# Block sums of the MLP weights: by DMA additions from DRAM to DRAM during the attention, instead of by GpSimd during merge and MLP

## The chip, the cores and the metric

One NeuronCore of one Trainium2 chip runs the whole program. The metric is device microseconds of one execution, the median of several runs.

## The reference

One layer of a decoder in float32, with S = D = 1024 and DFF = 4096:

```python
h = rms_norm(x);  proj = h @ w_in          # q k v | conv x,B,C | q_m | 3 gates
y_attn = (differential attention, 8 heads, causal) @ w_attn_o
y_conv = (B * causal conv3(C * x_c)) @ w_conv_o
y_mem  = (cross attention over 256 memory rows) @ w_mem_o
x = x + (g_a*y_attn + g_c*y_conv + g_m*y_mem) @ w_o
h2 = rms_norm(x, norm_mlp_g)
x = x + square(relu(h2 @ w_mlp_in)) @ w_mlp_out
```

## The kernel before

Every float32 product is made as three TensorE (PE) matmuls of rounded parts: each operand is split into hi (a cast, `whi`, `whh`, on ACT) and lo (raw minus hi, `wlo`, on DVE or GpSimd/POOL), and hi·hi, hi·lo, lo·hi are added up. A weight is so first loaded into a "raw" tile by SP's queue, then split, then used.

The program in order of time in the profiled execution:

- 0 to 245 us: memory attention and the norm of x.
- 245 to 1256: the attention, 64 steps s (8 heads of 8 row blocks). Each step issues the score, transpose and value products of a block, and `qkv(s + 1)` (L648 to L676), whose small norm chain on POOL is sq, r (two instructions, in `rstd_of`), qd; the transposes of qd are PE's next work for that block. Between these pieces PE runs matmuls of a stream (`fill_steps`), the conv and gate projections of x. At a change of head, `load_head` loads and casts the next head's weights (`rawh`, then `whh`).
- 1256 to 1536: the merge, three branches b = 2, 1, 0 of eight columns (`branch_steps`). At the last column of a branch `prep` loads and splits the next branch's operand (`rawx`, then `x`); at the very last, the first third of W_o.
- 1536 to 1632: W_o and the residual; 1632 to 1731: the row norm, and the transposes for the MLP.
- 1731 to 1997: the MLP's first product (`up`), and to 2314 the second. Each is a 2x2 block scheme of the Strassen family: seven block products instead of eight for each of 8 groups g. Of the seven weight blocks of each product four are sums of quarters of the weight matrix. The operands X are made by `second_sums` and `put`; the first product's results are squared (`out1`), combined and stored to `u_dram`, which the second product reads.

The weight sums are made by the program itself. `sum_jobs` (L530) has 32 jobs for w_mlp_in: two SP loads of 256 KB into one tile `sumw` of the "raw" pool (three buffers, shared with every `raw`, `rawh` and `rawx`), four POOL additions or subtractions, a 512 KB store from POOL's queue to `sw1_dram`. Eight are called in the attention (one in each head, at s % 8 == 6), 24 in the merge (L618, after each column's second half). `sum_jobs2` (L547) does the same for w_mlp_out, 32 jobs beside `up`, in the three "t" buffers that `tt` and `tu` use.

What sets the order: PE's instructions are pinned in the order of the program, and so are all SP loads (`pin_load`). The order on DVE, ACT and POOL is made by the tile framework's scheduler, which may put an instruction earlier than it is written.

Of the kernel before, what the change touches and what calls it, by code (L numbers as in the profile page):

```python
# [60 lines left out]
def tile_hybrid_block(ctx: ExitStack, tc: tile.TileContext, x, mem, norm_mix_g, norm_mem_g, w_in, b_gate,  # L61
# [103 lines left out]
    def row(name, src, n):  # L165
        t = const.tile([P, n], F32, name=name)
        nc.scalar.dma_start(t, src.unsqueeze(0).broadcast_to([P, n]))
        return t

    def rstd_of(ss, n, width, tag):  # L170

        r = sm.tile([P, width], F32, tag=tag, bufs=3, name="r")
        G.tensor_scalar(r, ss, 1.0 / n, EPS, op0=ALU.mult, op1=ALU.add)  # L173
        G.tensor_tensor(out=r, in0=r, in1=mhalf[:, 0:width], op=ALU.pow)  # L174
        return r


# [109 lines left out]
    z_dram = dram.tile([3, KT, P, S], F32, name="z_dram")  # L287

    NG = DFF // 512
    sw1_dram = dram.tile([NG, P, 4, 4, 256], F32, name="sw1_dram")  # L290
    sw2_dram = dram.tile([NG, P, 4, 2, 512], F32, name="sw2_dram")


    memT = [[slot(f"memT{c}{kq}", shape=(P, 4, MEM)) for kq in range(2)] for c in "hl"]
# [229 lines left out]
                yield  # L524


    def sub_(out, a, b):
        G.tensor_tensor(out=out, in0=a, in1=b, op=ALU.subtract)  # L528

    def sum_jobs():  # L530

        w1b = w_mlp_in.rearrange("(h k p) (c g n) -> h k p c g n", h=2, k=4, p=P, c=2, n=256)
        for g in range(NG):
            for k in range(4):
                z = rawt("sumw", (P, 2, 2, 256))
                for h in range(2):
                    load(z[:, h], w1b[h, k, :, :, g, :])
                a11, a21, a12, a22 = z[:, 0, 0], z[:, 0, 1], z[:, 1, 0], z[:, 1, 1]
                G.tensor_tensor(out=a22, in0=a21, in1=a22, op=ALU.add)  # L539
                sub_(a21, a11, a21)  # L540
                sub_(a11, a22, a11)
                sub_(a12, a12, a11)

                G.dma_start(sw1_dram[g, :, :, k, :], z.rearrange("p a b n -> p (a b) n"))
                yield

    def sum_jobs2(tile):  # L547
        w2b = w_mlp_out.rearrange("(h g j p) (d m n) -> h g j p d m n", h=2, j=2, p=P, d=2, n=256)
        for g in range(NG):
            for j in range(2):  # L550
                for m in range(2):
                    z = tile().rearrange("p a (b n) -> p a b n", b=2)
                    for h in range(2):
                        load(z[:, h], w2b[h, g, j, :, :, m, :])
                    b11, b12, b21, b22 = z[:, 0, 0], z[:, 0, 1], z[:, 1, 0], z[:, 1, 1]
                    sub_(b11, b12, b11)
                    sub_(b12, b22, b12)
                    sub_(b22, b22, b11)
                    sub_(b21, b21, b22)

                    G.dma_start(sw2_dram[g, :, :, j, m * 256:(m + 1) * 256], z.rearrange("p a b n -> p (a b) n"))
                    yield
# [33 lines left out]
    def branch_steps(b):  # L596
        w_src = srcs[b][0]
        w, z = ready.pop(b)
        for c in range(KT):
            gt = rowt("gt")  # L600
            load(gt, z_dram[b, c])
            A.activation(gt, gt, AF.Sigmoid, bias=bg[:, b * KT + c:b * KT + c + 1])
            wn = load_w(w_src[:, (c + 1) * P:(c + 2) * P], P, "wh", V) if c + 1 < KT else None
            if b == 2:
                merged[c] = slot("merged", F32, tag="m")
            if c == KT - 1:
                if b:
                    prep(b - 1)
                else:
                    ready["wo"] = load_wo(0)  # L610
            if b == 0:
                mh, ml = mT.add("mT", ("fw" if c < 4 else "s", "m" if c else "s"))
            for hf in range(2):
                sl = slice(hf * 512, (hf + 1) * 512)
                ps = ps_sc(512) if hf else ps_mm()
                yield from mm3_steps(ps, w, z.half(hf))
                if hf:
                    run(jobs, 1)  # L618
                if b == 2:
# [220 lines left out]
    for s in range(ns):  # L840

        if s == 0:
            fill = (16, 8, 8, 1)
        elif s == ns - 1:
            fill = (10, 40, 10, 8)
        else:
            fill = (17, 7, 8, 4)
        qk_transposes(s)
        run(stream, fill[0])
        if s == 0:  # L850
            p_transposes(nq - 1)
# [12 lines left out]
        values(s)  # L864
        if s % 8 == 6:
            run(jobs, 1)
        run(stream, fill[3])
    run(stream, 24)
# [135 lines left out]
    def second_sums(t):  # L1004
        ra, rb = rows.pop(t - 4), rows.pop(t)
        tt, tu = blk("tt", "t"), blk("tu", "t")
        sub(G, tt[:, 0], rb[:, 0], ra[:, 0])
        sub(V, tu[:, 0], rb[:, 1], rb[:, 0])
        sub(G, tt[:, 1], rb[:, 1], tt[:, 0])
        sub(G, tu[:, 1], ra[:, 1], tt[:, 1])  # L1010
        tsum[t] = rb, tt, tu

    def second_half(t):
# [6 lines left out]

    B = {}

    def out1(g, name, src, addend=None):

        t = B[g, name] = blk(name, "c")
        if addend is None:
            A.activation(t, src, AF.Relu)
            V.tensor_tensor(out=t, in0=t, in1=t, op=ALU.mult)
        else:
            add(V, t, src, addend)  # L1030
            V.scalar_tensor_tensor(out=t, in0=t, scalar=0.0, in1=t, op0=ALU.max, op1=ALU.mult)
# [6 lines left out]
    def up(n):  # L1038
# [16 lines left out]
            out1(g, "c11", ps, B.pop((g, "s", 1)))  # L1055
            put_u(1, g, B[g, "c11"])
        if i == 7:
            out1(g, "c22", ps1[g, "Z"], B.pop((g, "s", 7)))
            put_u(4, g, B[g, "c22"])
        if i == 4:  # L1060
            out1(g, "c21", ps)
            put_u(2, g, B[g, "c21"])
        if i == 3:
            out1(g, "c12", ps, B.pop((g, "s", 6)))
            c11, c12, c21, c22 = (B.pop((g, c)) for c in ("c11", "c12", "c21", "c22"))

            add(V, c22, c12, c22)
# [13 lines left out]
        first_half(t)  # L1081
    split1(1)
    alloc_x(6, 5, 7, 4, 3)
    jobs = sum_jobs2(lambda: blk("sumw", "t"))
    for n in range(len(seq1)):
        if 9 < n < 48 and n % 7 != 3:
            run(jobs, 1)
        load1(n + 4)
        split1(n + 2)
        if n < 4:  # L1090
            load_rows(n)
            load_rows(4 + n)
            second_sums(4 + n)
        up(n)
        if n < 4:
            second_half(4 + n)

    run(jobs)


    w2v = w_mlp_out.rearrange("(h g j p) (d n) -> h d g p j n", h=2, j=2, p=P, d=2)
# [3 lines left out]
    def load2(n):  # L1105
        if n < len(seq2):
# [4 lines left out]
            if i in (1, 2, 3):  # L1111
                h, d = {1: (0, 0), 2: (1, 0), 3: (1, 1)}[i]
                load(w, w2v[h, d, g])
            else:
                load(w, sw2_dram[g, :, {5: 0, 7: 1, 4: 2, 6: 3}[i]])

    def split2(n):
        if n < len(seq2):
# [24 lines left out]
    for n, (i, g) in enumerate(seq2):  # L1143
# [7 lines left out]
        for m in range(4):  # L1151
# [4 lines left out]
                             stop=g == NG - 1 and k == 1 and q == 2, skip_group_check=True)  # L1156
            if i == 3 and g == NG - 1:
                t = sn[6][m // 2]
                add(V, t[:, m % 2, :], ps[m // 2][:, m % 2, :], t[:, m % 2, :])
                put_out(0, 1, m // 2, t, (m % 2,))  # L1160
        if g < NG - 1:
            continue
# [51 lines left out]
```

## Time and profile before

| | |
|---|---|
| median of 3 runs | 2313.75 us (2308.81 to 2314.91) |
| the profiled execution | 2315.68 us |
| its span in the profile | 2313.9 us |
| PE busy | 2219.8 us (96%) |
| DVE, ACT, POOL busy | 1213.6, 953.1, 811.6 us |
| bytes moved by DMA | 338.29 MB, mean 146 GB/s |

PE is busy nearly throughout, so a shorter time needs fewer idle stretches of PE, or less time at its lower clock, and a row on another engine counts only where PE waits for it. The granted clock ("PEclk") is 1.00 at 2.4 GHz; a window of time that shows 0.75 ran half of its time at 1.2 GHz.

### The profile page before, as it was taken

The page shows a single profiled execution, that of the slowest core. Times are in us where ns is not written, and L with a number is a line of the kernel's source. Part 1 is how long each engine was busy: PE and PEld are TensorE (multiplying, and loading weights), DVE is VectorE, ACT ScalarE, POOL GpSimd, SP SyncE. Part 2 cuts the span into 40 slices and gives each one's busy share as a digit, 9 for nine tenths or more (in the row PEclk, how much of TensorE's full clock was granted, in tenths as well). Part 3 has the DMA queues.
Part 4 walks back from the last instruction along what each step waited for, and adds up shares of the span by engine and source line. Part 5 has one row for each costly group of instructions (what it writes and reads, how often), then busy time and mean ns, then how long its engine had stood idle before and what let it go on. Part 6 is the DMA issues. An engine that isn't in the chain of part 4 may idle for free.

```text
span 2313.9 us, 31608 instructions
## 1 busy us (share of the span) xinstructions
PE 2219.8 (96%) x11472; PEld 1919.3 (83%) x11472; DVE 1213.6 (52%) x2200; ACT 953.1 (41%) x2190; POOL 811.6 (35%) x1084
## 2 busy tenths in 40 slices
PE   6999999999999999999999999989679999999999
PEld 6999888888888888888887887879568888788887
DVE  6755455555555555555556343342447676664452
ACT  5544445454545454444545232331222323354341
POOL 5422233333233232333334444641417788100000
PEclk9999999999999999999999999999789999999999
DMA  7412121222212121222214775752828999886660
GB/s 201 128 61 63 46 79 59 67 80 66 72 51 91 42 87 42 75 63 67 80 64 143 238 238 174 226 157 90 294 83 307 331 338 350 292 304 219 219 227 37
DMA packets 242748, 338.29 MB, mean 146 GB/s; under 512 B 20256, under 2 KB 182048, under 8 KB 242592
## 3 DMA queue, kind: packets, MB, share of 16 engines
q1 hardware_dynamic: 206128, 239.64, 32.5%
q0 software_dynamic: 19584, 71.31, 8.2%
q10 hardware_dynamic: 16880, 25.33, 3.1%
q8 instruction: 90, 1.47, 0.3%
q14 instruction: 66, 0.54, 0.1%
HBM read 235.56 MB, written 100.66 MB: 145 GB/s over the span
## 4 chain that ended last, share of the span: by engine, by line
PE 74%; DMA 10%; DVE 6%; POOL 4%; issue 3%; ACT 2%; SPq 1%; ACTq 0%; POOLq 0%; DVEq 0%
PE ps_mm L89 37%; PE X L89 14%; PE Z L89 11%; PE ps_sc L89 7%; DMA sumw<-in_w_mlp_in_dram 3%; PE ps_tr L93 3%; PE ps_tr L89 3%; POOL sumw L528 2%; DVE wlo L184 1%; DMA raw<-in_w_attn_o_dram 1%; DMA xr<-xn_dram 1%; SPq L98 1%; POOL merged L623 1%; DMA sw_dram<-sumw 1%; POOL sumw L539 1%
## 5 line engine op out<-in xcount | busy, mean ns | idle before, releaser
L89 PE MATMUL ps_mm<-hT,whi 128*128 128x512 f32 x1536 | 490.3, 400 | 1.7 <-DVE vst L668 1.7
L89 PEld LDWEIGHTS ps_mm<-hT,whi 128*128 128x128 f32 x1536 | 279.0, 189 | 53.3 <-DVE vst L668 4.7
L89 PE MATMUL ps_mm<-hT,wlo 128*128 128x512 f32 x768 | 301.7, 393 | 0.0
L89 PE MATMUL ps_mm<-whh,hT 128*128 128x384 f32 x1024 | 276.4, 340 | 1.9 <-DVE inner L475 1.9
L528 POOL TENSOR_TENSOR sumw<-sumw 128x256 f32<-128x256 f32 x224 | 215.0, 961 | 40.5 <-DMA sumw<-in_w_mlp_out_dram 29.6
L89 PEld LDWEIGHTS ps_mm<-whh,hT 128*128 128x128 f32 x1024 | 186.3, 188 | 7.2 <-DVE inner L475 3.7
L184 DVE TENSOR_TENSOR wlo<-raw,whi 128x256 fp32r<-128x256 f32 (+2 forms) x169 | 123.9, 749 | 121.4 <-ACT whi L202 108.6
L89 PE MATMUL X<-w,u 128*128 128x512 f32 x768 | 174.6, 389 | 0.0
L184 POOL TENSOR_TENSOR wlo<-raw,whi 128x512 fp32r<-128x512 f32 (+2 forms) x95 | 116.3, 1230 | 162.9 <-ACT whi L202 161.9
L89 PE MATMUL ps_mm<-whl,hT 128*128 128x384 f32 x512 | 171.4, 335 | 0.0
L89 PEld LDWEIGHTS X<-w,u 128*128 128x128 f32 x768 | 144.2, 188 | 29.9
L670 POOL TENSOR_TENSOR sq<-qk 128x256 f32<-128x256 f32 x64 | 42.6, 665 | 356.9 <-ACT qk L665 356.5
L89 PEld LDWEIGHTS ps_mm<-hT,wlo 128*128 128x128 f32 x768 | 144.7, 188 | 27.5
L202 ACT CAST whi<-raw 128x512 fp32r<-128x512 f32 (+2 forms) x264 | 127.0, 530 | 77.5 <-PE ps_mm L89 13.1
L174 POOL TENSOR_TENSOR r<-r,mhalf 128x1 f32<-128x1 f32 (+1 forms) x186 | 132.8, 714 | 14.4
L914 DVE TENSOR_TENSOR u<-uraw,u 128x1024 fp32r<-128x1024 f32 x56 | 72.1, 1288 | 118.9 <-ACT u L920 118.5
L89 PE MATMUL Z<-w,u 128*128 128x512 f32 x576 | 131.7, 390 | 1.6 <-DVE snap L917 1.6
L173 POOL TENSOR_SCALAR r<-ss 128x1 f32<-128x1 f32 (+1 forms) x186 | 39.7, 214 | 255.2 <-ACT ps_tr L764 106.0
L89 PEld LDWEIGHTS Z<-w,u 128*128 128x128 f32 x576 | 108.0, 188 | 24.8 <-DVE snap L917 2.4
L89 PE MATMUL ps_mm<-x,whi 128*128 128x512 f32 x384 | 120.6, 395 | 4.0 <-DVE x L184 3.3
L920 ACT CAST u<-uraw 128x1024 fp32r<-128x1024 f32 x56 | 59.0, 1054 | 156.9 <-PE X L89 74.6
L89 PE MATMUL ps_sc<-x,whi 128*128 128x512 f32 x384 | 118.8, 391 | 1.1 <-DVE gt L622 1.1
(236 smaller groups left out, 4836.1 us busy)
## 6 DMA issues: line engine op xcount, KB each, us to landing
sw_dram<-sumw POOLq DMA_DIRECT2D x64, 512.0 KB, 5.8
raw<-in_w_in_dram SPq DMA_DIRECT2D x56, 512.0 KB, 3.8
u_dram<-c POOLq DMA_DIRECT2D x56, 512.0 KB, 6.0
uraw<-u_dram SPq DMA_DIRECT2D x56, 512.0 KB, 5.3
sumw<-in_w_mlp_in_dram SPq DMA_DIRECT2D x64, 256.0 KB, 4.1
w1raw<-sw_dram SPq DMA_DIRECT2D x32, 512.0 KB, 6.6
sumw<-in_w_mlp_out_dram SPq DMA_DIRECT2D x64, 256.0 KB, 6.0
w2raw<-sw_dram SPq DMA_DIRECT2D x32, 512.0 KB, 4.3
```

Source lines behind the costliest of these rows:

```text
L89: return cls.pin(nc.tensor.matmul(*a, **kw))
L93: return cls.pin(nc.tensor.transpose(*a, **kw))
L98: return pin_load(nc.sync.dma_start(dst, src))
L173: G.tensor_scalar(r, ss, 1.0 / n, EPS, op0=ALU.mult, op1=ALU.add)
L174: G.tensor_tensor(out=r, in0=r, in1=mhalf[:, 0:width], op=ALU.pow)
L184: eng.tensor_tensor(out=lo, in0=raw, in1=f(hi), op=ALU.subtract)
L202: A.copy(out=hi[:, a:b, :], in_=raw[:, k0 + a:k0 + b, :])
L528: G.tensor_tensor(out=out, in0=a, in1=b, op=ALU.subtract)
L539: G.tensor_tensor(out=a22, in0=a21, in1=a22, op=ALU.add)
L670: G.tensor_tensor(out=sq, in0=qk, in1=qk, op=ALU.mult)
L914: eng.tensor_tensor(out=out, in0=a, in1=b, op=ALU.subtract)
L920: A.copy(out=hl[:, 0], in_=raw)
```

## The change

All 64 jobs go. In their place POOL's queue issues 16 DMAs of 4.19 MB each (a quarter of a weight matrix) from DRAM to DRAM, eight plain copies and eight additions (`accum_op` add: the destination gets source plus destination). One is issued every third step of the attention, at s = 1, 4, ..., 46, and pinned behind the last `pow` that has been written (`last_norm`). Each matrix needs four sums; each begins as a copy of a quarter or of an earlier sum, and quarters are added to it:

| s | 1 | 4 | 7 | 10 | 13 | 16 | 19 | 22 |
|---|---|---|---|---|---|---|---|---|
| w_mlp_in | copy r to z0 | copy r to z1 | add s to z0 | add q to z1 | copy z0 to z2 | add q to z2 | copy z2 to z3 | add t to z3 |

and w_mlp_out the same way at s = 25 to 46 (its additions to z0 and z1 are q and s, its z2 begins as z1). Rows are 8 KB for w_mlp_in, 2 KB for w_mlp_out, and 64 KB where both sides are whole sums. A DMA that reads or adds to what an earlier one wrote waits for it, and the wait stands on POOL, which issues it.

Only sums can be made so, no differences; the signs are moved to other operands: `put` negates two of the X blocks, and a few additions become subtractions. The loads of the sums into `w1raw` now have runs of 1 KB where they had 4 KB. `load_w` in `branch_steps` no longer names DVE for all of the lo parts, so they alternate between DVE and POOL.

```diff
     def rstd_of(ss, n, width, tag):
...
-        G.tensor_tensor(out=r, in0=r, in1=mhalf[:, 0:width], op=ALU.pow)
+        last_norm[0] = G.tensor_tensor(out=r, in0=r, in1=mhalf[:, 0:width], op=ALU.pow)
...
-    sw1_dram = dram.tile([NG, P, 4, 4, 256], F32, name="sw1_dram")
-    sw2_dram = dram.tile([NG, P, 4, 2, 512], F32, name="sw2_dram")
+    sw1 = [dram.tile([D // 2, DFF // 2], F32, name=f"sw1{i}") for i in range(4)]
+    sw2 = [dram.tile([DFF // 2, D // 2], F32, name=f"sw2{i}") for i in range(4)]
...
     def sum_jobs():
 
-        w1b = w_mlp_in.rearrange("(h k p) (c g n) -> h k p c g n", h=2, k=4, p=P, c=2, n=256)
-        for g in range(NG):
-            for k in range(4):
-                z = rawt("sumw", (P, 2, 2, 256))
...
+        def go(out, in_, op=ALU.bypass):
+            after(G.dma_start(out, in_, accum_op=op), last_norm[0])
+
+        a = [w_mlp_in[h * 512:(h + 1) * 512, c * 2048:(c + 1) * 2048] for c in range(2) for h in range(2)]
+        b = [w_mlp_out[h * 2048:(h + 1) * 2048, d * 512:(d + 1) * 512] for h in range(2) for d in range(2)]
+        for (q, t, r, s), z in ((a, sw1), ((b[0], b[2], b[1], b[3]), sw2)):
+            for i, src, op in ((0, r, 0), (1, r, 0), (0, s, 1), (1, q if z is sw1 else s, 1), (2, z[0 if z is sw1 else 1], 0),
+                               (2, q, 1), (3, z[2], 0), (3, t, 1)):
+                if z is sw2 and (i, op) == (0, 1):
+                    src = q
+                go(z[i], src, ALU.add if op else ALU.bypass)
                 yield
...
-            wn = load_w(w_src[:, (c + 1) * P:(c + 2) * P], P, "wh", V) if c + 1 < KT else None
+            wn = load_w(w_src[:, (c + 1) * P:(c + 2) * P], P, "wh") if c + 1 < KT else None
...
-                if hf:
-                    run(jobs, 1)
...
-        if s % 8 == 6:
+        if s % 3 == 1:
             run(jobs, 1)
...
-                load(r, sw1_dram[g, :, {6: 0, 7: 1, 3: 2, 5: 3}[i]])
+                load(r, sw1[{5: 0, 7: 1, 6: 2, 3: 3}[i]].rearrange("(k p) (g n) -> g p k n", p=P, n=256)[g])
...
-        A.copy(out=hi, in_=src)
-        sub(V, lo, src, f(hi))
+        if i in (4, 5):
+            A.activation(hi, src, AF.Copy, scale=-1.0)
+            V.scalar_tensor_tensor(out=lo, in0=src, scalar=-1.0, in1=f(hi), op0=ALU.mult, op1=ALU.subtract)
+        else:
+            A.copy(out=hi, in_=src)
+            sub(V, lo, src, f(hi))
...
-            sub(V, c11, c22, c11)
-            sub(V, c21, c21, c11)
+            V.scalar_tensor_tensor(out=c11, in0=c22, scalar=-1.0, in1=c11, op0=ALU.mult, op1=ALU.subtract)
+            V.scalar_tensor_tensor(out=c21, in0=c21, scalar=-1.0, in1=c11, op0=ALU.mult, op1=ALU.subtract)
...
-    jobs = sum_jobs2(lambda: blk("sumw", "t"))
     for n in range(len(seq1)):
-        if 9 < n < 48 and n % 7 != 3:
-            run(jobs, 1)
```

The order moves at three places. First POOL inside a step of the attention, before: four `sumw` operations of a job stand between the members of the norm chain (sq, r, r, qd).

```order
L539 TENSOR_TENSOR sumw<-sumw 128x256
L670 TENSOR_TENSOR sq<-qk 128x256
L528 TENSOR_TENSOR sumw<-sumw 128x256
L173 TENSOR_SCALAR r<-ss_3891 128x4
L528 TENSOR_TENSOR sumw<-sumw 128x256
L174 TENSOR_TENSOR r<-r,mhalf 128x4
L528 TENSOR_TENSOR sumw<-sumw 128x256
L675 TENSOR_TENSOR qd<-qk,r 128x256
L544 DMA sw_dram<-sumw 512x1x256
```

The same place after, around one of the 16 DMAs (`sw_92`): the chain sq, r, r, qd has nothing between, and the DMA stands behind the next norm and ahead of the next step's sq.

```order
L648 TENSOR_TENSOR sq<-qk 128x256
L175 TENSOR_SCALAR r<-ss_6043 128x4
L176 TENSOR_TENSOR r<-r,mhalf 128x4
L653 TENSOR_TENSOR qd<-qk,r 128x256
L186 TENSOR_TENSOR wlo<-raw,whi 128x512
L175 TENSOR_SCALAR r<-ss 128x1
L176 TENSOR_TENSOR r<-r,mhalf 128x1
L532 DMA sw_92<-in_w_mlp_in_dram 512x2048
L648 TENSOR_TENSOR sq<-qk 128x256
```

What moved: the job's arithmetic is gone, and one DMA issue, which may carry a wait for an earlier DMA, stands ahead of sq. Second ACT at the change of head in step s = 14, before: the casts of the next head's weights (`whh`) come among the exponentials `e` of that step.

```order
L777 ACTIVATE osl<-ps_tr,sg 128x128
L644 CAST whh<-rawh 128x384
L723 ACTIVATE e,sums<-ps_sc,negm 128x896
L644 CAST whh<-rawh 128x384
L723 ACTIVATE e,sums<-ps_sc,negm 128x896
L644 CAST whh<-rawh 128x384 x2
L665 COPY qk<-ps_mm 128x256
L667 CAST vst<-ps_mm 128x128
L644 CAST whh<-rawh 128x384
```

After, the casts but the first come behind the whole step:

```order
L622 CAST whh<-rawh 128x384
L701 ACTIVATE e,sums<-ps_sc,negm 128x896 x2
L643 COPY qk<-ps_mm 128x256
L645 CAST vst<-ps_mm 128x128
L724 CAST aT<-ps_tr 128x512
L724 CAST aT<-ps_tr 128x384
L502 COPY z<-ps_mm 128x512
L739 ACTIVATE o<-ps_tr,sums 128x128
```

What moved: three or more `whh` casts that stood ahead of the step's `qk` copy now stand behind its `o`. Third POOL at the end of the merge, before: `sumw` operations and a store stand between the last additions into `merged`, which W_o reads.

```order
L544 DMA sw_dram<-sumw 512x1x256
L623 TENSOR_TENSOR merged<-merged,gt 128x512 x3
L539 TENSOR_TENSOR sumw<-sumw 128x256
L623 TENSOR_TENSOR merged<-merged,gt 128x512
L528 TENSOR_TENSOR sumw<-sumw 128x256 x3
L544 DMA sw_dram<-sumw 512x1x256
L623 TENSOR_TENSOR merged<-merged,gt 128x512 x2
```

After:

```order
L601 TENSOR_TENSOR merged<-merged,gt 128x512 x2
L186 TENSOR_TENSOR wlo<-raw,whi 128x384
L601 TENSOR_TENSOR merged<-merged,gt 128x512 x2
L186 TENSOR_TENSOR wlo<-raw,whi 128x384
L186 TENSOR_TENSOR wlo<-raw,whi 128x256
L601 TENSOR_TENSOR merged<-merged,gt 128x512 x7
L186 TENSOR_TENSOR wlo<-raw,whi 128x384 x4
```

What moved: nothing but the `wlo` parts that `load_w` now gives to POOL stands between the last `merged` additions.

## Rows read from the trace of the kernel before

**Rows 1.** The profile page, parts 1, 2 and 3 (queue: packets, MB, share of 16 engines).

```profile
PE 2219.8 (96%) x11472; PEld 1919.3 (83%) x11472; DVE 1213.6 (52%) x2200; ACT 953.1 (41%) x2190; POOL 811.6 (35%) x1084
...
PEclk9999999999999999999999999999789999999999
...
GB/s 201 128 61 63 46 79 59 67 80 66 72 51 91 42 87 42 75 63 67 80 64 143 238 238 174 226 157 90 294 83 307 331 338 350 292 304 219 219 227 37
...
q0 software_dynamic: 19584, 71.31, 8.2%
```

**Rows 2.** Windows: us, busy (xcount) of PE, PEld, DVE, ACT, POOL, PEclk, DMA share, GB/s.

```profile
245.00:1256.00 1011.00, 990.25 (x5205) 862.17 (x5205) 553.42 (x1352) 488.65 (x1346) 334.60 (x499) 1.00 0.21 67
...
1431.00:1456.00 25.00, 20.99 (x82) 15.68 (x81) 16.14 (x22) 10.51 (x19) 11.14 (x12) 0.93 0.74 243
...
1530.00:1550.00 20.00, 13.52 (x57) 11.58 (x57) 9.46 (x15) 7.12 (x16) 11.52 (x12) 0.74 0.51 159
...
1632.00:1731.00 99.00, 67.52 (x282) 53.95 (x283) 42.46 (x50) 29.39 (x44) 22.71 (x21) 0.79 0.49 174
1731.00:1985.00 254.00, 254.00 (x1122) 210.37 (x1121) 173.37 (x123) 76.76 (x77) 187.08 (x205) 1.00 0.93 325
1985.00:1997.00 12.00, 8.28 (x30) 6.38 (x29) 9.11 (x8) 3.35 (x4) 2.13 (x4) 0.86 0.67 225
```

**Rows 3.** Waits of PE, 245 to 1256 us: waited for, us in total, times, longest.

```profile
PE ps_tr L93 <- POOL qd L675: 7.3, 8, 1.0
```

**Rows 4.** Timeline of POOL in one attention step: start us, us, instruction, [idle before].

```profile
300.35 0.74 POOL L528 TENSOR_TENSOR sumw<-sumw 128x256 f32<-128x256 f32 x1
...
303.14 0.73 POOL L528 TENSOR_TENSOR sumw<-sumw 128x256 f32<-128x256 f32 x1
303.83 0.61 POOL L675 TENSOR_TENSOR qd<-qk,r 128x256 f32<-128x256 f32 x1
304.38 0.88 POOL L544 DMA_DIRECT2D sw_dram<-sumw  x1
```

**Rows 5.** Timeline of PE at the merge's last change of branch.

```profile
1442.65 0.50 PE L89 MATMUL ps_mm<-x,whi 128*128 128x512 f32 x1 [1.99 <-DVE x L184]
```

**Rows 6.** Waits of SP's queue, 1344 to 1545 us.

```profile
SPq L98 <- DMA sw_dram<-sumw: 41.3, 10, 9.2
```

**Rows 7.** Timeline of POOL at the end of the merge.

```profile
1534.52 1.27 POOL L623 TENSOR_TENSOR merged<-merged,gt 128x512 f32<-128x512 f32 x1
1535.74 3.07 POOL L528 TENSOR_TENSOR sumw<-sumw 128x256 f32<-128x256 f32 x3
...
1539.77 0.74 POOL L544 DMA_DIRECT2D sw_dram<-sumw  x1 [0.96 <-POOL sumw L528]
```

**Rows 8.** Timeline of PE at the start of W_o.

```profile
1542.92 0.69 PE L89 MATMUL ps_mm<-whi,mT 128*128 128x384 f32 x1 [3.63 <-ACT whi L202]
```

**Rows 9.** Timeline of PE where the MLP's second product begins.

```profile
1990.26 0.50 PE L89 MATMUL X<-x4h,w 128*128 128x512 f32 x1 [3.72 <-ACT snap L1053]
```

**Rows 10.** DMA issues: out<-in, queue, count, KB each, median us from issue to landing.

```profile
sw_dram<-sumw POOLq DMA_DIRECT2D x64, 512.0 KB, 5.8
raw<-in_w_in_dram SPq DMA_DIRECT2D x56, 512.0 KB, 3.8
...
rawh<-in_w_in_dram SPq DMA_DIRECT2D x64, 192.0 KB, 2.8
...
w1raw<-in_w_mlp_in_dram SPq DMA_DIRECT2D x24, 512.0 KB, 8.0
```

**Rows 11.** Timeline of ACT in step 14: the last cast of the next head's weights.

```profile
480.38 0.52 ACT L644 CAST whh<-rawh 128x384 fp32r<-128x384 f32 x1
```

**Rows 12.** Timeline of PE: the first matmul that uses those weights.

```profile
489.60 0.42 PE L89 MATMUL ps_mm<-whh,hT 128*128 128x384 f32 x1
```

**Rows 13.** Groups by line and form, DVE: busy us, mean ns of one, idle before.

```profile
L914 DVE TENSOR_TENSOR c<-c,c 128x1024 f32<-128x1024 f32 x24 | 38.3, 1598 | 0.4
L1031 DVE SCALAR_TENSOR_TENSOR c<-c 128x1024 f32<-128x1024 f32 x24 | 37.9, 1578 | 0.1
```

More of the change, by code (lines that the diff above doesn't have):

```diff
@@ L168, in row @@
         return t
+    last_norm = [None]
     def rstd_of(ss, n, width, tag):
@@ L524, in fill_steps @@
                 yield
-    def sub_(out, a, b):
-        G.tensor_tensor(out=out, in0=a, in1=b, op=ALU.subtract)
     def sum_jobs():
-        w1b = w_mlp_in.rearrange("(h k p) (c g n) -> h k p c g n", h=2, k=4, p=P, c=2, n=256)
-        for g in range(NG):
-            for k in range(4):
-                z = rawt("sumw", (P, 2, 2, 256))
[L536 to L544, printed above, removed]
-                yield
@@ L547, in sum_jobs2 @@
[L547 to L562, printed above, removed]
+        def go(out, in_, op=ALU.bypass):
+            after(G.dma_start(out, in_, accum_op=op), last_norm[0])
@@ L1008, in second_sums @@
         sub(V, tu[:, 0], rb[:, 1], rb[:, 0])
-        sub(G, tt[:, 1], rb[:, 1], tt[:, 0])
-        sub(G, tu[:, 1], ra[:, 1], tt[:, 1])
+        sub(G, tt[:, 1], tt[:, 0], rb[:, 1])
+        add(G, tu[:, 1], ra[:, 1], tt[:, 1])
         tsum[t] = rb, tt, tu
@@ L1021, in tile_hybrid_block, with out1 @@
     B = {}
-    def out1(g, name, src, addend=None):
+    def out1(g, name, src, addend=None, sign=1):
         t = B[g, name] = blk(name, "c")
         if addend is None:
-            A.activation(t, src, AF.Relu)
+            A.activation(t, src, AF.Relu, scale=float(sign))
             V.tensor_tensor(out=t, in0=t, in1=t, op=ALU.mult)
@@ L1030, in out1 @@
             add(V, t, src, addend)
-            V.scalar_tensor_tensor(out=t, in0=t, scalar=0.0, in1=t, op0=ALU.max, op1=ALU.mult)
+            V.scalar_tensor_tensor(out=t, in0=t, scalar=0.0, in1=t, op0=ALU.max if sign > 0 else ALU.min,
+                                   op1=ALU.mult)
     def put_u(i, g, t):
@@ L1057, in up @@
         if i == 7:
-            out1(g, "c22", ps1[g, "Z"], B.pop((g, "s", 7)))
+            out1(g, "c22", ps1[g, "Z"], B.pop((g, "s", 7)), -1)
             put_u(4, g, B[g, "c22"])
         if i == 4:
-            out1(g, "c21", ps)
+            out1(g, "c21", ps, sign=-1)
             put_u(2, g, B[g, "c21"])
@@ L1065, in up @@
             c11, c12, c21, c22 = (B.pop((g, c)) for c in ("c11", "c12", "c21", "c22"))
-            add(V, c22, c12, c22)
+            sub(V, c22, c22, c12)
             sub(V, c12, c11, c12)
-            sub(V, c11, c22, c11)
-            sub(V, c21, c21, c11)
+            V.scalar_tensor_tensor(out=c11, in0=c22, scalar=-1.0, in1=c11, op0=ALU.mult, op1=ALU.subtract)
+            V.scalar_tensor_tensor(out=c21, in0=c21, scalar=-1.0, in1=c11, op0=ALU.mult, op1=ALU.subtract)
             for k, t in ((5, c22), (7, c12), (6, c11), (3, c21)):
@@ L1096, in tile_hybrid_block @@
             second_half(4 + n)
-    run(jobs)
     w2v = w_mlp_out.rearrange("(h g j p) (d n) -> h d g p j n", h=2, j=2, p=P, d=2)
@@ L1114, in load2 @@
             else:
-                load(w, sw2_dram[g, :, {5: 0, 7: 1, 4: 2, 6: 3}[i]])
+                load(w, sw2[{5: 0, 7: 1, 6: 2, 4: 3}[i]].rearrange("(g j p) n -> g p j n", j=2, p=P)[g])
     def split2(n):
@@ L1158, in tile_hybrid_block @@
                 t = sn[6][m // 2]
-                add(V, t[:, m % 2, :], ps[m // 2][:, m % 2, :], t[:, m % 2, :])
+                sub(V, t[:, m % 2, :], t[:, m % 2, :], ps[m // 2][:, m % 2, :])
                 put_out(0, 1, m // 2, t, (m % 2,))
@@ L1170, in tile_hybrid_block @@
                 sn[i].append(t)
-                add(V if i == 7 else G, t, t, xq.pop((*{1: (0, 0), 6: (0, 1), 7: (1, 1)}[i], jj)))
+                xr = xq.pop((*{1: (0, 0), 6: (0, 1), 7: (1, 1)}[i], jj))
+                if i == 1:
+                    add(G, t, t, xr)
+                else:
+                    sub(V if i == 7 else G, t, xr, t)
         if i in (2, 7):
@@ L1175, in tile_hybrid_block @@
                 t = sn[k][jj]
-                add(V, t, ps2["Z"][jj], t)
+                if i == 2:
+                    add(V, t, ps2["Z"][jj], t)
+                else:
+                    sub(V, t, t, ps2["Z"][jj])
                 put_out(th, d, jj, t)
```

## The prediction

> **What bounds the kernel now.** I read the page first, then windows by stage, then PE's waits in the stages where PE is not full, and last the engines and queues that those waits name. The page says PE 96% busy [rows 1], so anything moved off POOL, DVE or SP is worth only what PE waits for it. The windows [rows 2] show where that can be. The first product of the MLP, 1731 to 1985, has the most traffic (325 GB/s, DMA share 0.93) and POOL busy 187 us, 32 of the jobs among it, yet PE is busy 254.00 of 254.00 at clock 1.00: relief there gives nothing back inside the stage. The transition, 1632 to 1731, is the emptiest (67.52 of 99, clock 0.79), but no sum runs there before or after, so it stays. What is left is four places where a job of the sums stands near an idle PE: the attention, the last change of branch, the start of W_o, and the start of the second product.
>
> **What is removed, place by place.**
>
> Attention: a job's four operations stand between sq, r and qd, three of them 0.73 to 0.74 us each, and qd comes out at 303.83 [rows 4]. PE waited for qd 8 times, 7.3 us [rows 3], once for each of the eight jobs there. The order shows the chain with nothing between now: gain up to 7.3.
>
> Change of branch, 1431 to 1456: PE is idle 25 − 20.99 = 4.0 us, and the clock 0.93 costs (1 − 0.93) × 25 = 1.7 more. PE waits for the next operand's parts [rows 5]; these wait for raw buffers, which SP cannot fill until a job's store has left: SP's queue waited 41.3 us, 10 times, for that [rows 6]. Up to 5.7.
>
> Start of W_o, 1530 to 1550: idle 20 − 13.52 = 6.5 us. The clock 0.74 says that 0.26 × 20 × 2 = 10.4 us ran at 1.2 GHz; one wait of 3.63 [rows 8] is surely among them and counted already, so what the matmuls in it lose is (10.4 − 3.6) / 2 = 3.4. On POOL three `sumw` operations (3.07 us) and a store stand between the last `merged` additions [rows 7], and W_o's own raw loads stand behind the jobs' loads on SP. Up to 9.9.
>
> Start of the second product, 1985 to 1997: idle 3.7 (all in one wait for `snap` [rows 9]) and (1 − 0.86) × 12 = 1.7. The DMA engines were at 0.93 just before. The 32 jobs there move 1 MB each, 33.6 MB of 254 us × 325 GB/s = 82.6 MB, so the stage falls to some 190 GB/s and what `snap` waits for comes sooner. Up to 5.4.
>
> Together 7.3 + 5.7 + 9.9 + 5.4 = 28.3. Some of each boundary must remain: after the last `merged` addition (1.27 us [rows 7]) a cast and a subtraction stand before PE in any case. I leave 3 for that: **gain 25**.
>
> **What is added.** Sixteen DMAs. The trace has no DRAM-to-DRAM transfer and no DMA addition, so I bound them. POOL's queue moved 71.31 MB in 8.2% of 16 × 2313.9 us [rows 1]: 23.5 GB/s for one engine, 376 for 16. One pass of 4.19 MB takes 11.2 us. A copy is one pass (read and write overlap) or two: 11.2 to 22.3. An addition reads two and writes one: 22.3 to 33.5, the far bounds being one pass, 11.2, and rows that go one after another, 32 for each engine at the 5.8 us of a landing [rows 10], 186 us. I take 22 to 33, because POOL's rows of 1 KB and more went at that rate. All sixteen then take 8 × (11.2 + 22.3) = 268 to 8 × (22.3 + 33.5) = 446 us. A slot is three steps of 1011 / 64 = 15.8 us [rows 2], 47.4 us, so they have 758 us, beside 67 GB/s of other traffic. They fit, and the last ends long before 1731, where sums are first read.
>
> What they delay: SP's loads share the engines with them. The attention's `raw` loads land in 3.8 us, while loads of the same size under the MLP's crowd take 8.0 [rows 10]. A `raw` load is issued a whole unit of 48 matmuls ahead, and none of PE's waits in that stretch names a `raw` part now, so 4.2 us more is hidden; I put 2 us for what isn't. At a change of head there is less room: the last `whh` cast ends at 480.9 [rows 11] and PE needs the weights at 489.60 [rows 12], 8.7 us. Only two of the seven changes, in s = 14 and s = 38, have a large DMA issued just ahead (a copy with 64 KB rows at s = 13 and 37); all others end before the loads if a copy takes under some 24 us and an addition under some 50. A copy issued at the end of s = 13, near 245 + 14 × 15.8 = 466, ends at 477 to 488. The `rawh` loads then land in about 2.8 × 8.0 / 3.8 = 5.9 us each, and the new order also has the casts behind most of the step, so the slack may go. Cost 0 to 21 (two times the 10.6 of rival H); I take 2 × 3 = 6, because only the tail of a copy meets the loads. Together **cost 8**.
>
> Issuing costs POOL about 0.9 us each [rows 4] in place of four operations and an issue: nothing, in steps where POOL is busy a third of the time [rows 2]. Loads of the sums in runs of 1 KB cost nothing: loads from w_mlp_in have such runs already and take 8.0 us in the crowd that goes away, and PE there was full. The sign edits cost nothing: DVE's two forms take 1578 and 1598 ns [rows 13], ACT scales in the same pass. The merge's `wlo` parts on POOL cost nothing where POOL is relieved of 24 jobs; uncovered they would return one wait of rows 5, 2 us, for each branch.
>
> **The sum.** 2315.68 − 25 + 8 = 2298.7 for an execution like the profiled one, which lies 1.9 above the median of the runs. Forecast against that median: **2297 us**.
>
> **Rivals.**
>
> W, other causes behind the boundaries. In the MLP the sums' traffic goes, but at both merge places the loads themselves and the split chain may be the next late thing, and the SP waits [rows 6] only their echo. Then half of the 21.0 us there stays: 7.3 + 10.5 − 8 = 9.8 gained, 2304 us. For it: PE waits there name DVE and ACT [rows 5, 8], which have their own queues. Against: both sit behind tiles that jobs hold.
>
> H, the head changes give more back. The highest slice of the page shows 350 GB/s [rows 1]. If that is a limit on bytes read and written together, a copy is 8.39 MB, 24.0 us; issued at 466 it ends at 490, and `rawh` loads that must wait for it start where PE already needs the weights. The eight (1.57 MB) then need 4.2 us at 376 GB/s, 5.9 for the last landing and a cast of 0.5: 10.6 late, twice. 2297 − 6 + 21 = 2312 us. [...] Against H: the loads need only 8.7 us less than they have, and the queues of the MLP run side by side.
>
> S, **slower**: an addition takes longer than its slot. Three of the copies (s = 19, 37, 43) read what the addition of one slot before wrote, and the wait stands on POOL ahead of the next step's sq, at the head of the chain whose end is qd [rows 4]; PE then has no qd and stops. With an addition of A us POOL is held A − 47.4 + 2 us three times (2 for issue and notice). At 60 us that is 15 each, 2297 + 45 = 2342 us; at 80, 2401. It decides from 3 × (A − 45.4) = 17, A = 51. For it: no row here prices an addition, and the far bound is 186. Against: 51 us is more than twice the passes that the rate of rows 1 gives.
>
> That the sums are not done beside the attention at all would need the scheduler to hold them; they are pinned step by step, and the new order has them there. I give it nothing.
>
> **How the numbers follow.** A measurement of this kernel tells about 0.3% (7 us) from no change: faster is below 2307, slower above 2321. My forecast 0.62; W 0.12; H 0.10; S 0.16. The forecast's own range is 2285 (nothing left of any wait, no cost: 2313.75 − 28.3) to 2307 (waits half left, cost 8), W 2299 to 2309, H 2307 to 2318, S anything over 2313. Faster: 0.59 of the forecast and 0.07 of W make 0.66. Slower: 0.15 of S, 0.02 of H and 0.02 of the forecast and W (small losses where I put nothing), 0.19. Same: the 0.15 left. The range from 2283, two below the least that the sum allows, to 2325 holds all but the larger part of S, about 0.13, and a few in a hundred below.
>
> **What would show it.** Right: no wait of PE for qd in the attention; SP's queue without waits for a store of sums in the merge; the windows 1431 to 1456 and 1530 to 1550 fuller, with clock near 1.00; no idle 3.7 before the second product; copies landing in 11 to 22 us, additions in 22 to 33. For H: `whh` casts waiting for `rawh` in s = 14 and 38, and PE idle behind them. For S: POOL idle before a DMA issue at s = 19, 37, 43, and PE waits for qd of over 10 us right behind. What would make it all wrong is a price of the additions outside of 11 to 50 us, or a PE loss in the transition, which I left untouched.

## The result and the profile after

The changed kernel takes 2283.78 us (2283.37 to 2284.44, 4 runs) where the kernel before took 2313.48 beside it: ratio 0.9875, 95% interval [0.9858, 0.9892]. The forecast was 2297 with a range of 2283 to 2325: the right side, but 30 us were gained and 17 forecast, so terms of the sum were mis-sized.

The page of the changed kernel, to be read against [rows 1]: POOL has lost over a quarter of its work, PE is idle 73 us of the span where it was 94, and POOL's queue has doubled its share of the DMA engines.

```profile
span 2282.7 us, 30985 instructions
PE 2209.3 (97%) x11472; PEld 1917.8 (84%) x11472; DVE 1170.1 (51%) x2167; ACT 953.5 (42%) x2190; POOL 576.0 (25%) x813
...
q0 software_dynamic: 24192, 104.86, 16.5%
```

Its windows, cut at the matmuls that begin and end the stretches of [rows 2] (columns as there): the change of branch, the start of W_o, the first MLP product and the change to the second. The first two are full now and at full clock. The first product lost 160 us of POOL's work and 39% of its traffic, and takes the same 254 us.

```profile
1420.00:1439.00 19.00, 19.00 (x86) 15.73 (x85) 9.98 (x14) 10.91 (x19) 9.01 (x8) 1.00 0.44 138
1511.00:1521.00 10.00, 10.00 (x56) 9.65 (x55) 5.91 (x8) 4.23 (x10) 4.35 (x4) 1.00 0.15 45
1703.00:1957.00 254.00, 253.46 (x1118) 209.89 (x1119) 148.31 (x126) 79.44 (x80) 24.78 (x47) 1.00 0.57 197
1957.00:1965.00 8.00, 6.90 (x31) 5.39 (x30) 5.30 (x5) 1.01 (x1) 1.33 (x3) 1.00 0.67 214
```

PE's waits in the attention of the changed kernel: no row for qd [rows 3] any more, and one that was not there, for `whl`.

```profile
PE ps_tr L93 <- DVE o L744: 3.6, 1, 3.6
PE ps_mm L89 <- DVE whl L186: 3.1, 2, 1.5
PE ps_tr L93 <- DVE e L710: 2.0, 5, 1.3
PE ps_mm L89 <- DVE inner L477: 1.9, 8, 0.3
```

PE issues the same 11472 matmuls in the same order in every kernel here, so the time between two given matmuls can be compared from trace to trace. The table names each stretch by its times in the kernel before; the experiments' rows are told of below.

| us between the same matmuls | attention 245–1250 | first columns 1250–1344 | branch 1430–1456 | 1510–1530 | W_o 1530–1550 | transition 1625–1731 | second product 1985–1997 |
|---|---|---|---|---|---|---|---|
| before | 1005.2 | 93.8 | 25.9 | 20.0 | 20.1 | 106.1 | 12.2 |
| changed | 995.6 | 93.7 | 19.0 | 18.6 | 10.1 | 107.7 | 8.0 |
| before_alt | 1003.2 | 93.6 | 24.8 | 18.6 | 20.1 | 107.0 | 8.0 |
| before_no1 | 991.6 | 94.1 | 19.0 | 18.6 | 10.1 | 106.5 | 8.0 |
| before_no2 | 1004.7 | 93.5 | 27.5 | 19.0 | 20.1 | 105.4 | 8.0 |
| after_v | 996.0 | 93.7 | 19.0 | 18.6 | 10.1 | 110.4 | 8.0 |
| free | 992.1 | 94.2 | 19.0 | 18.6 | 10.1 | 104.6 | 8.0 |
| late | 990.5 | 92.8 | 19.0 | 18.6 | 10.1 | 107.4 | 8.0 |
| shift | 1038.8 | 92.7 | 19.0 | 18.6 | 10.1 | 106.4 | 8.0 |
| displaced | 1039.2 | 92.8 | 19.0 | 18.6 | 10.1 | 109.3 | 8.0 |
| burst | 1038.0 | 93.2 | 19.0 | 18.6 | 10.1 | 106.4 | 8.0 |
| every | 1069.8 | 93.6 | 19.0 | 18.6 | 10.1 | 109.1 | 8.0 |
| chunks | 1012.2 | 99.9 | 19.0 | 18.6 | 10.1 | 106.0 | 8.0 |

The first two rows place the gain: attention 9.6, branch 6.9, the column behind it 1.4, W_o 10.0, second product 4.2, and 1.6 given back in the transition. The transition, whose code and data paths the experiments leave alone, comes out between 104.6 and 110.4; differences of that size there are scatter, not effects.

### The profile page after: what moved, and what is told of

The parts are those of the page before. It is cut to its first block, busy times and chain, and to the rows that moved or that the text cites. A ratio compares the mean times of both kernels' runs of the same rounds, so it can differ in the third digit from the quotient of the medians.

```text
span 2282.7 us, 30985 instructions
## 1 busy us (share of the span) xinstructions
PE 2209.3 (97%) x11472; PEld 1917.8 (84%) x11472; DVE 1170.1 (51%) x2167; ACT 953.5 (42%) x2190; POOL 576.0 (25%) x813
## 3 DMA queue, kind: packets, MB, share of 16 engines
q1 hardware_dynamic: 187696, 206.07, 27.6%
## 4 chain that ended last, share of the span: by engine, by line
PE 89%; DVE 4%; DMA 3%; ACT 2%; issue 1%; POOL 1%; SPq 0%; ACTq 0%; DVEq 0%; POOLq 0%
PE ps_mm L89 45%; PE X L89 15%; PE Z L89 12%; PE ps_sc L89 11%; PE ps_tr L93 3%; PE ps_tr L89 3%; DMA xr<-xn_dram 1%; ACT qh L671 1%; DVE ql L676 1%; DVE whl L186 0%; DVE wlo L186 0%; DMA xt<-in_x_dram 0%; DMA rawh<-in_w_in_dram 0%; DMA memt<-in_mem_dram 0%; DMA xn_dram<-xn 0%
## 5 line engine op out<-in xcount | busy, mean ns | idle before, releaser
L186 POOL TENSOR_TENSOR wlo<-raw,whi 128x512 fp32r<-128x512 f32 (+2 forms) x128 | 145.1, 1139 | 244.1 <-ACT whi L204 241.6
L89 PEld LDWEIGHTS ps_mm<-hT,wlo 128*128 128x128 f32 x768 | 145.0, 189 | 27.5
L186 DVE TENSOR_TENSOR wlo<-raw,whi 128x512 fp32r<-128x512 f32 (+2 forms) x136 | 109.5, 810 | 64.3 <-ACT whi L204 63.5
L701 ACT ACTIVATE e<-ps_sc,negm 128x256 f32<-128x256 f32 (+7 forms) x128 | 94.1, 740 | 32.5 <-DVE negm L698 32.5
```

What stands on the lines that cost most here:

```text
L89: return cls.pin(nc.tensor.matmul(*a, **kw))
L186: eng.tensor_tensor(out=lo, in0=raw, in1=f(hi), op=ALU.subtract)
L701: A.activation(e[:, 0:n], sc[:, 0:n], AF.Exp, scale=-1.0, bias=negm[:, c:c + 1], accum_out=sums[:, c:c + 1])
```

## Experiments: what the gain consists of

**before_no1**, the kernel before without the jobs for w_mlp_in.

```diff
-    jobs = sum_jobs()
+    jobs = iter(())
-                load(r, sw1_dram[g, :, {6: 0, 7: 1, 3: 2, 5: 3}[i]])
+                load(r, w1v[0, 1, g])
```

> The kernel before without the 32 jobs for w_mlp_in (its sums are left out, a quarter is read in their place); the 32 jobs beside the MLP's first product stay. Theory, from the places where PE's lead rose: attention 9, change of branch and 1515 8.4, start of W_o 10.1, together 27.5: 2286 us. Rival (the boundaries have other causes, and only the attention's waits go): 2303.

2281.97 us, ratio 0.9860 [0.9846, 0.9875]. These 32 jobs alone carry the whole gain, and the attention gains 13.6 rather than 9. Both places of the merge come out to the tenth as in the changed kernel, and PE has no wait at all between 1390 and 1560. The rival falls, and with it the prediction's W. PE's waits in its attention:

```profile
PE ps_tr L93 <- DVE o L766: 4.9, 1, 4.9
PE ps_tr L93 <- DVE e L732: 3.4, 5, 1.5
PE ps_mm L89 <- DVE inner L475: 1.9, 8, 0.3
PE ps_mm L89 <- DVE vst L668: 0.5, 2, 0.2
PE ps_sc L89 <- DVE ql L698: 0.2, 1, 0.2
```

These are 10.9 us. In the kernel before the same list had 20.4: the 7.3 of [rows 3], 0.2 for ql, and these rows:

```profile
PE ps_tr L93 <- DVE e L732: 4.2, 9, 1.5
PE ps_tr L93 <- DVE o L766: 3.9, 1, 3.9
PE ps_mm L89 <- DVE inner L475: 1.9, 8, 0.3
PE ps_mm L89 <- DVE vst L668: 1.7, 7, 0.3
PE ps_tr L89 <- DVE aT L747: 1.2, 3, 0.4
```

So waits that name DVE (e, vst, aT) went with the jobs too (how the jobs fed them is not shown), and 9.5 us of waits less made 13.6 us: at each of the eight waits for qd, 0.8 to 1.0 us long, before_no1 and the changed kernel gain 1.1 to 1.2 on the kernel before, 9 us where the waits are 7.3.

**before_no2**, the same for w_mlp_out.

```diff
-    jobs = sum_jobs2(lambda: blk("sumw", "t"))
+    jobs = iter(())
-                load(w, sw2_dram[g, :, {5: 0, 7: 1, 4: 2, 6: 3}[i]])
+                load(w, w2v[0, 1, g])
```

> The kernel before without the 32 jobs for w_mlp_out beside the MLP's first product (its sums are left out, a quarter is read in their place). Theory: only the wait at the start of the second product goes, 4.8 us: 2308.7, although POOL loses some 150 us of work and the DMA engines 33.6 MB in that stage. Rival (the wait for snap has its cause in the chain of the last results): 2313.

2312.47 us, ratio 0.9996 [0.9986, 1.0005]: no difference. The stage loses the jobs' traffic and POOL's work, and nothing comes of it, as [rows 2] had said of the stage itself. At the start of the second product its trace has 8.0 for 12.2, as the theory has it; but so has before_alt, in which all these jobs run.

**before_alt**, the kernel before with one edit of the change, and **after_v**, the changed kernel without it.

```diff
-            wn = load_w(w_src[:, (c + 1) * P:(c + 2) * P], P, "wh", V) if c + 1 < KT else None
+            wn = load_w(w_src[:, (c + 1) * P:(c + 2) * P], P, "wh") if c + 1 < KT else None
```

> The kernel before with one edit of the change: load_w in branch_steps alternates DVE and POOL. Theory: 2313.5 within 2, since the jobs hold the raw buffers and POOL. Rival 1 (DVE was late): 2306 to 2309. Rival 2 (POOL, with sumw and the lo parts, becomes late): 2316 to 2320.

> The changed kernel with DVE named again for all lo parts of load_w in branch_steps. Theory (the merge's gain comes from the jobs that went, not from where the lo parts are made): 2283.8 within 1.5. Rival (part of the 6.9 us at the change of branch and of the 10.1 at the start of W_o is DVE's relief): 2287 to 2292, with PE waits for x or wlo from DVE between 1420 and 1530.

before_alt 2314.18, ratio 0.9989 [0.9977, 1.0001]; after_v 2287.01, ratio 0.9881 [0.9863, 0.9899], 3.2 us above the changed kernel. The theory's bound for after_v was missed and the rival's 2287 met, but not in the rival's place: the merge's four columns of the table are the same to the tenth, and PE waits for nothing between 1390 and 1560. The profiled executions differ by 4.3 us, 2.7 of it in the transition, where kernels with the same code differ by more, and 1.7 ahead of 245. So the edit is worth nothing in the merge without the jobs. With them it moves waits: before_alt loses 4.6 us between 1456 and 1510, where PE now waits 2.6 for `gt`, and gains 2.5 at the two places beside it; the medians agree. before_alt also has 8.0 where the kernel before has 12.2; its PE row there and that of the kernel before [rows 9] are the same wait at other lengths:

```profile
PE X L89 <- ACT snap L1053: 1.1, 1, 1.1
```

The wait of 3.7 us that the prediction put down to the sums' traffic is thus seen in the one execution of the kernel before, and not in another kernel with the same jobs. What made it is left open.

**free**, the changed kernel without the 16 DMAs.

```diff
-    jobs = sum_jobs()
+    jobs = iter(())
-                load(r, sw1[{5: 0, 7: 1, 6: 2, 3: 3}[i]].rearrange("(k p) (g n) -> g p k n", p=P, n=256)[g])
+                load(r, w1v[0, 1, g])
-                load(w, sw2[{5: 0, 7: 1, 6: 2, 4: 3}[i]].rearrange("(g j p) n -> g p j n", j=2, p=P)[g])
+                load(w, w2v[0, 1, g])
```

> The changed kernel without the 16 DMAs; where the MLP read a sum it reads a quarter of the weight matrix, so the sums are left out. It is the floor of what any way of making the sums beside other work can reach. Theory (the DMAs cost nothing but the order at two heads): as shift, 2281, within 1.5. Rival (sixteen transfers crowd the attention's loads or POOL everywhere): below 2278, with the attention's waits of PE shorter than in shift.

2281.34 us, ratio 0.9858 [0.9836, 0.9880]. The changed kernel is 2.4 us above its floor, 3.5 in the attention by the table. The theory's number holds, and the rival's does not: where the change put its DMAs, they cost hardly anything.

## Experiments: what the DMAs cost, and where

**shift**: the same DMAs at other steps, meant to take them away from the two heads where the changed kernel has its `whl` waits. It does that, but at s % 8 = 3 it also issues a DMA 14 us ahead of the first two weight loads of every change of head.

```diff
-        if s % 3 == 1:
+        if s % 8 in (0, 3):
```

> The 16 DMAs at s % 8 in (0, 3) in place of s % 3 == 1, so that none is issued just ahead of a head's weight loads, and ACT's order has the whh casts among the exponentials at every change of head again. In the changed kernel's trace PE's lead over the kernel before fell by 3.9 us after s = 14 and by 2.3 after s = 38, but had risen there by 2.5 and 1.0 just ahead, because the casts no longer stood before the exponentials. Theory (net cost of the two heads 1.4 + 1.3): 2281 us. Rival, the two falls are the whole cost and the rises have other causes: 2277.5. Rival, the heads are not the cause: 2284, as the changed kernel.

2327.23 us, ratio 1.0051 [1.0035, 1.0068]: slower than the kernel before, 43 us above the changed one, and none of the three expectations comes near. PE's longest group of waits in the attention, the wait at one of six places, then what ACT shows there:

```profile
PE ps_mm L89 <- ACT z L502: 33.4, 6, 7.7
```
```profile
459.98 0.69 PE L89 MATMUL ps_mm<-whh,hT 128*128 128x384 f32 x1 [7.72 <-ACT z L502]
```
```profile
458.81 0.51 ACT L622 CAST whh<-rawh 128x384 fp32r<-128x384 f32 x1 [9.98 <-DMA rawh<-in_w_in_dram]
459.34 0.58 ACT L502 COPY z<-ps_mm 128x512 f32<-128x512 f32 x1
```

POOL had issued an addition at 432.02, which lands at 458.5. The first load of the next head's weights (192 KB) is issued at 445.9 and lands at 458.8, after 12.9 us, not 2.8 [rows 10]; its cast waits 9.98 us at the head of ACT's queue, and behind it stands the copy of `z` out of the `ps_mm` tile, for which PE waits 7.72. The weights themselves are first used at 498.05. So the late load stopped PE 38 us before PE needed what it brought, through the order on ACT.

With this in view the changed kernel's trace shows the same delay, without harm. A `raw` load beside the addition of s = 22, and four `rawh` loads beside the copy of s = 13, issue to landing:

```profile
L98 SPq DMA_DIRECT2D raw<-in_w_in_dram x1: 368/368/368, 612.3 to 612.3; - x1
...
DMA to landing us min/median/max: 22.5/22.5/22.5
```
```profile
L98 SPq DMA_DIRECT2D rawh<-in_w_in_dram x4: 368/440/5152, 465.0 to 467.9; - x4
...
DMA to landing us min/median/max: 11.5/12.2/13.0
```

The first lands at 634.8 against 3.8 us alone. The copy that delays the second group was issued at 460.86 and landed 15.5 us later, at 476.3; the group lands at 478 to 480. No wait of PE in the attention names a `raw` part even so.

How the loads are held back can be read from the DMA packets, one for each row. Below are POOL's queue (q0) and SP's (q1) in three stretches, with packets, MB and share of the 16 engines: the addition of s = 22 with rows of 8 KB (623 to 631 us, changed kernel), an addition with rows of 2 KB (s = 31, 769 to 773, changed kernel), and the copy of s = 13 with rows of 64 KB (465 to 474, changed kernel).

```profile
q0 software_dynamic: 197, 1.61, 96.7%
q1 hardware_dynamic: 200, 0.10, 6.4%
```
```profile
q0 software_dynamic: 328, 0.67, 90.2%
q1 hardware_dynamic: 328, 0.17, 21.0%
```
```profile
q0 software_dynamic: 48, 3.15, 98.5%
q1 hardware_dynamic: 16, 0.01, 0.3%
```

In the first two stretches the queues moved row for row, whatever the bytes: 25 load rows of 512 B in a us beside rows of 8 KB, 82 beside rows of 2 KB. In the copy 16 load rows went between its third round of 16 rows and its last. Without a bulk DMA the same queue moved 767 rows in 2 us (606 to 608). So the loads were not shut out until the bulk DMA ended; they moved at the pace of its rows. Beside rows of 8 KB that came to nearly the same: the load of 612.3 landed at 634.8, the addition at 633.3. Beside rows of 2 KB it need not: the loads issued at 798.7 and 992.0, 5 us behind such additions, land 6.3 and 6.0 us before these do (the one of 763.6, 13 us behind its addition, 0.2 us after it).

**burst**: shift with each DMA cut into four pieces of 1 MB, issued together.

```diff
-                go(z[i], src, ALU.add if op else ALU.bypass)
+                n = z[i].shape[0] // 4
+                for p in range(4):
+                    rows = slice(p * n, (p + 1) * n)
+                    go(z[i][rows], src[rows], ALU.add if op else ALU.bypass)
                 yield
```

> The kernel shift with each DMA cut into four of 1 MB, all four issued at once. If an engine lets other queues in only when a DMA ends, a load waits for the rest of one piece, 7 us at most, and the six waits of 7.7 us in shift mostly go: 2285 to 2295. If it is the backlog on POOL's queue that holds the loads back, whatever its pieces, it is as shift: 2327.

2327.44 us, ratio 1.0055 [1.0037, 1.0073], as shift; the two `rawh` loads at the same place took 12.7 and 12.9 us.

```profile
457.42 0.51 ACT L625 CAST whh<-rawh 128x384 fp32r<-128x384 f32 x1 [9.86 <-DMA rawh<-in_w_in_dram]
```

So the end of one piece did not let the loads in: behind four pieces they took as long as behind the one DMA of shift (12.9 and 13.0). That they moved row for row through the whole backlog of POOL's queue is the author's reading from the three fences above, not shown for burst; cutting the DMAs left their rows as long as they were, and no run here cuts the rows.

**displaced**: shift with ACT's order at the heads of s = 14 and 38 pinned as the changed kernel has it.

```diff
-                A.copy(out=hi, in_=raw[:, k, :])
+                ins = A.copy(out=hi, in_=raw[:, k, :])
+                if h in (2, 5) and k0 + k >= 2:
+                    after(ins, last_qh[0])
```

> The kernel shift with ACT's order pinned at the heads of s = 14 and 38 as the changed kernel has it (six casts of each behind the step's last qh), and no large DMA near. Order theory: the displaced casts alone cost what the changed kernel pays, so 2283.8, the whl waits of some 1.5 us back at both. Collision theory (the copy on the engines at 461 to 476 delays the rawh loads): as shift, about 2281, no whl waits.

2328.99 us, ratio 1.0065 [1.0048, 1.0081]. It rests on shift, so the times expected of it fall with that; what was to be told apart can still be read against shift. The `whl` waits are back with no DMA near:

```profile
PE ps_mm L89 <- DVE whl L186: 3.1, 2, 1.5
```

and the `rawh` loads of the displaced casts land in 2.6 to 4.2 us. Between the same matmuls displaced differs from shift by −2.5 us at 470 to 480 and +4.0 at 490 to 500, and by −1.0 and +2.4 at the second head (850 to 860, 870 to 880; all in times of the kernel before). The changed kernel differs from free by the same four numbers. The displaced casts alone are enough for its loss there, net 1.5 us a head; the whole attention of displaced is only 0.4 above shift's, since its other stretches came out shorter.

**late**: the changed kernel with only the two copies of s = 13 and 37 moved, one step later.

```diff
-        if s % 3 == 1:
+        if s % 3 == 1 and s not in (13, 37) or s in (14, 38):
```

> The changed kernel with the two copies of s = 13 and 37 one step later, at 14 and 38, behind the head's loads. ACT's order is then that of all other heads. Theory: the eight rawh loads of those heads land in 3 us again, not in 12 to 13; PE's whl waits (1.5 twice) and the half clock behind them go, its waits for e come back: 2281 to 2283, at most 2.7 below the changed kernel. Rival (no net cost there): 2284.

2282.18 us (2278.14 to 2287.14), ratio 0.9860 [0.9843, 0.9878]. ACT's order is regular again, `rawh` lands in at most 4.8 us, the `whl` waits are gone (in the changed kernel the half clock followed only the first of them, 0.50 from 489.3 to 492.5), and the attention takes 990.5, 5 us less than the changed kernel and no more than free. In the times it is 1.6 below the changed kernel, within the spread of its own runs: better by its trace, not shown better by the clock.

```profile
DMA to landing us min/median/max: 2.4/2.8/4.8
```
```profile
PE ps_tr L93 <- DVE o L744: 3.5, 1, 3.5
PE ps_tr L93 <- DVE e L710: 3.4, 5, 1.5
PE ps_mm L89 <- DVE inner L477: 1.9, 8, 0.3
```

**every**: the DMAs one step apart.

```diff
-        if s % 3 == 1:
+        if 1 <= s <= 16:
```

> The changed kernel with the DMAs one step apart (s = 1 to 16). The sixteen took 313 us on the engines in the changed kernel's trace (copies 14 to 17, additions 22 to 28), and 16 steps are 253. Theory S of the prediction, as a test of its price: POOL stands before the dependent ones, about 13 us at the sixth, 7 at the seventh, 30 at the thirteenth, 8 and 6 at the last two, with sq, r and qd behind it, and PE loses most of it: 2335 to 2348. Rival (PE's matmuls of the stream cover the wait): 2284 to 2292.

2361.01 us, ratio 1.0201 [1.0185, 1.0217], 13 above the theory's upper end. POOL did stand before its dependent DMAs, but for 27.6 us in all (its rows first); ACT's wait for `rawh` is twice that (second fence), and PE lost its time behind ACT (third):

```profile
POOL sw L532 <- DMA sw<-in_w_mlp_out_dram: 18.7, 1, 18.7
...
POOL sw L532 <- DMA sw<-sw: 8.9, 3, 5.2
```
```profile
ACT whh L622 <- DMA rawh<-in_w_in_dram: 59.4, 8, 19.4
```
```profile
PE ps_mm L89 <- ACT whh L622: 27.4, 3, 17.7
PE ps_mm L89 <- ACT z L502: 26.7, 3, 17.2
PE ps_tr L89 <- DVE aT L725: 10.3, 1, 10.3
```

Only the last row follows a stop of POOL (18.7 us). The loss is real, its place is not the one that S named: 54 us come through delayed loads, 10 through POOL.

**chunks**: the changed kernel with each DMA in the same four pieces, but one piece a step in all 64 steps (the `yield` stands inside the loop).

```diff
-        if s % 3 == 1:
-            run(jobs, 1)
+        run(jobs, 1)
```

> Each of the 16 DMAs cut into four of 1 MB, one issued in each of the 64 steps. Theory, from shift and every: a load on SP's queue that is issued while a DMA of POOL's queue is under way lands only when that one is through; 1 MB takes 3.6 to 7 us, so rawh lands in at most 10, no PE wait for z or whh of over 2 us, and the time is that of free, 2281, within 2. Rival (each change of head now meets a DMA, and each meeting costs what it cost in shift): 2290 or more.

2307.37 us, ratio 0.9965 [0.9952, 0.9979]. Of the landing the theory was right (`rawh` at most 8.5 us), of the time the rival: every change of head now meets pieces, `rawh` lands in 3.6 at the median, and PE waits there for e and twice for `whh` itself. The attention takes 1012.2, and the first columns of the merge 99.9 instead of 93.7: a load of the merge's operand, issued at 1264.7 beside one of the last pieces, lands after 10.1 us, and PE waits 3.2 us for that operand.

```profile
PE ps_tr L93 <- DVE e L713: 13.0, 9, 4.0
PE ps_tr L93 <- ACT whh L625: 5.0, 2, 2.8
```
```profile
DMA to landing us min/median/max: 2.5/3.6/8.5
```

## Why the prediction was right, and where it was off

- **The number.** 2283.78 lies below the 2285 that the forecast gave as the least its sum allows, nothing left of any wait and no cost at all. That it is inside the range is owed to the 2 us put below that bound: the mechanism was right, but that the range holds the time is luck.
- **Where the sums cost PE.** Right for the attention and both merge places: before_no1, which only takes the jobs away, gets the whole gain there. The terms: branch up to 5.7, measured 6.9; W_o up to 9.9, measured 10.0 and 1.4 in the column ahead. The 3 us that "must remain" were the first step that failed: nothing is left, PE is full in both stretches. The lower clock in these terms is in the trace of the kernel before: granted 0.50 from 1543 to 1547, with matmuls of 128x384 starting 0.32 us apart, 1.2 columns in a ns, and 0.17 apart behind it at 1.00. W falls with this; its sum also halved 21.0 us, the second product's 5.4 among them, although the merge's two places that it speaks of come to 15.6.
- **Attention, gain 7.3.** The second: it counted only the waits named qd. Without the jobs the attention takes 13 us less (free 13.1, before_no1 13.6), because the same jobs fed waits that name e, vst and aT, and a stop of PE cost a little more than its own length (9 us for the 7.3).
- **Cost 8.** Measured 2.4 by the times, 3.5 by the attention's traces, about 3 of it at the two heads. The prices were well bounded: the eight copies landed in 14.8 to 18.9 us, the eight additions in 24.0 to 30.8. The place was right too, the heads of s = 14 and 38, and so was half of the reason: displaced shows that the new order of the casts makes the loss without late loads. But the step "the `rawh` loads then land in about 5.9 us each" was wrong: 11.5 to 13.5, and `raw` up to 22.5 where 8.0 was put. Wrong too were the margins at the other heads, 24 us for a copy and 50 for an addition. The first two loads of a head are issued some 22 us before the others, so the margins were 14 and 29: the addition issued at 413.4 landed at 439.6, 3.0 us ahead of the next head's first load at 442.6; the one issued at 793.4 landed at 824.2, 1.7 us behind such a load at 822.5. That these loads met no more than the tail of a transfer is luck; in shift they met half of it.
- **Start of the second product, 5.4.** 4.2 in the trace, but not shown to be the sums' doing (before_alt, before_no2).
- **Nothing from relief of the MLP's first product, nothing for the signs and for load_w.** Right: 254 us before and after; ACT's casts into X (128x512) took 596 to 597 ns with the sign and 584 to 594 without; free and before_no1, with and without the sign edits, differ by 0.6 us.
- **H.** Loads that land only about when a bulk transfer is through are what shift, burst and every show (`rawh` up to 15.5, 14.4 and 33.7 us where 2.8 is the median before); in the changed kernel, with 13.5 at most, this only makes loads late that have time. The reason it gave, the 350 GB/s of [rows 1] as a limit on bytes read and written together, fails: it would have made a copy 24.0 us, and the copies landed in 14.8 to 18.9, 8.39 MB read and written, 444 to 567 GB/s.
- **S.** An addition took 24.0 to 30.8 us of a slot of some 46, so POOL never waited in the changed kernel. The 2 us for issue and notice stand in no row; in every the issues themselves took 0.62 to 1.93. every also shows that too close a spacing loses as much as S said, but by the loads first.

Together: attention −0.7 forecast, 9.6 gained; boundaries 18 forecast, 22.5 gained.

## What to carry to other kernels

Work that only shares an engine's queue with a short chain can cost more than the waits that name the chain, here 13 us against 7.3: leave it out once and take the difference between the same matmuls. A bulk DMA on another queue did not slow the loads here by its share of the bytes: rows went one for one (200 of 512 B beside 197 of 8 KB), so such a load landed close to the end of the bulk DMA's backlog, 634.8 against 633.3. Place the DMA by the issue times of the loads that have the least slack, and compare that slack with the whole transfer. A load that is needed late can still stop PE early, if its cast stands on its engine ahead of something PE needs: 7.72 us at 459.98 in shift, for weights used at 498.05.

## What the runs showed that was not expected

- Issuing the same 16 DMAs at other steps of the attention changed the kernel by 43 us, from 2283.78 to 2327.23, more than the change itself gained.
- A copy from DRAM to DRAM of 4.19 MB landed in 14.8 to 18.9 us, an addition in 24.0 to 26.2 with rows of 8 KB and in 26.7 to 30.8 with rows of 2 KB.
- At one change of head loads of 192 KB took 12.9 and 13.0 us behind 4 MB in one DMA, and 12.7 and 12.9 behind the same in four.
- Two DMA queues moved nearly equal numbers of rows, 328 of 512 B against 328 of 2 KB in 4 us, and 200 of 512 B against 197 of 8 KB in 8 us.
